# Forming the low parts of the projection weights with adding DMAs instead of a VectorE subtraction

## The chip, the core and the metric

The kernel runs on one core of a Trainium2 chip. The metric is device time in microseconds of one execution. A core has a matrix engine (PE; its weight loads are shown as PEld), VectorE (DVE), ScalarE (ACT), GpSimd (POOL) and SyncE (SP), each working through its own queue in order and waiting at semaphores, and 16 DMA engines that all queues share.

## The reference

One decoder layer over 1024 tokens of width 1024, in float32. Cut to what matters here:

```
u = rms_norm(x, ln_g)
z = u @ w_in                       # 1024 x 7168: seven groups of 8 column blocks of 128
c_val, c_glu, c_gate, hq, hf, hi, hg = split(z)
y_conv = (silu(layer_norm(conv31(c_val * sigmoid(c_glu)))) @ w_pw2 + b) * silu(c_gate)
y_hgrn = rms_norm(gated linear recurrence of hq, hf, hi in chunks) * silu(hg)
h = x + concat(y_conv, y_hgrn) @ w_out
h = h + sigmoid(rms_norm(h) @ w_pg) * (p @ w_pp)
out = rms_norm(h)
```

## The kernel before

Every large product is made of three matmuls in the rounded type float32r: each operand is split into `hi`, the operand rounded to float32r, and `lo`, the operand minus `hi`; then hi·hi + hi·lo + lo·hi are summed in PSUM. So a weight block needs its hi and its lo before its product can begin: the first matmul reads `w..h`, and the third already `w..l`.

The stages: a start (load `p`, `x` and the parameters, project `p` into `pe_d`, normalise and transpose `x` into the tiles `uh`, `ul`); the z stage, which makes `z` block by block, with the convolution and the recurrence of each head woven between; the pointwise projection; the output projection; the gated embedding.

In the z stage a weight block is 128 columns of `w_in`, 512 KB, in SBUF as 128 partitions of 1024 numbers. `ztile(idx)` prepares block `wz<idx>` (48 of them), and `values` prepares two blocks `wv_0`, `wv_1` for two heads at a time (8 in all). Both call `prep`: SP loads the block into a tile of tag `raw`, ACT writes `hi` by a copy, and DVE writes `lo` by a subtraction. The tags `raw`, `hi` and `lo` of the pool `wp` have three buffers each. So the load of a block waits until the block three before it has been split, and the split of a block waits until PE has finished the product of the block three before it. All of this stands at a raised priority (`high_priority(2000)`), so the scheduler places it early.

The order on each engine is set by the tile framework's scheduler, with offsets from the kernel: the last steps of a head (`ro`, `on`, `ot`) and of a convolution group (`ry`, `yn`) are placed later by hand. `rstd_of` makes the factors `rx` (rows of x), `ry` (convolution) and `ro` (heads) with two small POOL instructions each; the head's factor goes POOL `ro`, ACT `on`, PE transposes `ot`.

At the start SP's queue holds, in this order, the loads of `p`, `wpp`, the first block `wz8`, rows of `x` (`xt`), three more blocks `wz0`, `wz32`, `wz48`, more rows of `x`, and then the small parameter rows (`prow`: `conv_w` with 31 rows of 4 KB, and eight more, the last of them `lb_logits`). The transposes `pt` on PE need all of `prow`, and PE's work on `x` stands behind `pt`.

Of the kernel before, what the change touches and what calls it, by code (L numbers as in the profile page):

```python
# [16 lines left out]
P = 128  # L17
T = 1024          # tokens
D = 1024          # model width
G = 8             # channel groups, heads, 128-row blocks of T and D  # L20
TAPS = 31
PAD = TAPS - 1
H = 512           # half a row of 1024: one PSUM bank of float32
EPS = 1e-6
# Order of the work of each head and channel group: projections of the GLU gate (u), conv value
# (c), forget gate (f), query (q), values of two heads (v), output gate (g); conv (C); HGRN (H).
ORDER = ("ucfgqvCH", "ucfgqCH") * (G // 2)
# How much later than traced the scheduler takes work that waits on a chain of small steps.
LATER_STATS, LATER_CONV, LATER_HEAD = 50, 330, 240
# columns of the transposed parameter table  # L30
R_CB, R_CG, R_CBETA, R_BPW, R_L0, R_L1, R_ON, R_LN, R_PE = range(TAPS, TAPS + 9)
# [4 lines left out]
def trunk_kernel(ctx: ExitStack, tc: tile.TileContext, x, p, ln_g, w_in, conv_w, conv_b,  # L36
# [25 lines left out]

    # ---------------------------------------------------------------- constants
    ident = cst.tile([P, P], F32, name="ident")
# [5 lines left out]

    # per-channel parameters, channels on partitions
    par = cst.tile([P, G, NR], F32, name="par")
# [3 lines left out]
    def load_params(work):  # L76
        rows = work.tile([NR, D], F32, name="prow")
        nc.sync.dma_start(rows[0:TAPS, :], conv_w[0])
        for r, ap in ((R_CB, conv_b), (R_CG, cnorm_g), (R_CBETA, cnorm_b), (R_BPW, b_pw2),
                      (R_ON, onorm_g), (R_LN, ln_g), (R_PE, pe_norm_g)):  # L80
            nc.sync.dma_start(rows[r:r + 1, :], ap)
        nc.sync.dma_start(rows[R_L0:R_L0 + 2, :], lb_logits)
        pt = bank("t", "pt")
        for g in range(G):
            nc.tensor.transpose(pt[:, g * NR:(g + 1) * NR], rows[:, g * P:(g + 1) * P],
                                ident[:NR, :NR])
        nc.vector.tensor_copy(par, pt[:, :G * NR].rearrange("p (g r) -> p g r", r=NR))
        # lower bound: first row of the softmax over the layers
        l0, l1 = par[:, :, R_L0], par[:, :, R_L1]
        mx = cst.tile([P, G], F32, name="lmx")  # L90
        e0 = cst.tile([P, G], F32, name="le0")
        e1 = cst.tile([P, G], F32, name="le1")
        nc.vector.tensor_tensor(mx, l0, l1, op=ALU.max)
        nc.vector.tensor_tensor(e0, l0, mx, op=ALU.subtract)
        nc.vector.tensor_tensor(e1, l1, mx, op=ALU.subtract)
        nc.scalar.activation(e0, e0, AF.Exp)
        nc.scalar.activation(e1, e1, AF.Exp)
        nc.vector.tensor_tensor(e1, e0, e1, op=ALU.add)
        nc.vector.reciprocal(e1, e1)
        nc.vector.tensor_tensor(lbt, e0, e1, op=ALU.mult)  # L100
        nc.vector.tensor_scalar(oml, lbt, -1.0, 1.0, op0=ALU.mult, op1=ALU.add)
# [10 lines left out]
    def split(hi, lo, src):  # L112
        nc.scalar.activation(hi, src, AF.Copy)
        nc.vector.tensor_tensor(lo, src, hi.bitcast(F32), op=ALU.subtract)

    def prep(src, shape, name):
        """A weight block: loaded, and split exactly into two float32r parts."""
        raw = wp.tile(shape, F32, tag="raw", name=name)
        nc.sync.dma_start(raw, src)
        hi = wp.tile(shape, F32R, tag="hi", name=name + "h")  # L120
        lo = wp.tile(shape, F32R, tag="lo", name=name + "l")
        split(hi, lo, raw)
        return hi, lo

    def colblock(w, c0):
        return w[:, c0:c0 + P].rearrange("(k p) c -> p k c", p=P)
# [3 lines left out]

    # ---------------------------------------------------------------- z phase
    uh = [[None] * G, [None] * G]
    ul = [[None] * G, [None] * G]
    with tc.tile_pool(name="st", bufs=1) as st:
        # layer embedding, projected: kept in DRAM until the gate is known
        KP = p.shape[1] // P
# [29 lines left out]
        def norm_x(hf, xs):  # L166
            """Normalised input of four token blocks, channels on partitions, split."""
            for k in range(G):
# [12 lines left out]
        load_params(st)  # L181
        # masks[l][s, col]: where the key s is one that the score column couples to, the columns
        # being those of the block of 32 that s lies in
        ones = st.tile([P, 4 * 48], F32, name="ones")
        nc.gpsimd.memset(ones, 1.0)

        def block_mask(dst, first, step_n, step_j, l):
            """Sets dst[s, n, j, i] where s is in the l keys from first + n step_n + j step_j."""
            src = ones[:, :dst.shape[1] * dst.shape[2] * l].rearrange(
# [9 lines left out]
        def own_block(name, mf):  # L199
            """The columns of each row's own block out of those of the four blocks of 32."""  # L200
            n = mf.shape[1] // 4
# [33 lines left out]
    def product(wh, wl, mh, ml, tag, name):  # L235
        """Two banks [128 columns of w, 512 tokens] of w^T m."""
        res = []
# [9 lines left out]
    def ztile(idx):  # L247
        with tc.high_priority(2000):
            wh, wl = prep(colblock(w_in, idx * P), [P, G, P], f"wz{idx}")
        return product(wh, wl, uh, ul, "z", f"z{idx}")  # L250

    def values(idx, vt):
        """Two column tiles of z with tokens on partitions."""
        with tc.high_priority(2000):
            ws = [prep(w_in[j * H:(j + 1) * H, idx * P:(idx + 2) * P]
                       .rearrange("(k p) c -> p k c", p=P), [P, 4, 2 * P], f"wv{idx}_{j}")
                  for j in range(2)]
# [22 lines left out]
    def hgrn(h, QD, K, F, vt, sgT):  # L280
        A, B = AT[h % 2], AB
        # Decayed scores. A level couples the later blocks of l tokens in a parent block to the
        # earlier ones: queries carry the decay since their block of l began (and over the
        # blocks in between), keys the decay until their block of l ends, so that every factor
        # is at most one.
        # Levels within blocks of 32: every block's scores take 48 columns, on its own 32
        # partitions, and go to B[s, chunk, t mod 32].
        blocks = T // 32

        def scores(l, rhs):  # L290
            pt = bank("t", f"sc{h}_{l}")
            pv = pt[:, :G * 48].rearrange("p (c w) -> p c w", c=G)
            for b in range(blocks):
# [4 lines left out]

        # Diagonal and pairs: the keys are the same.
        q01 = QD[:, :, :32].rearrange("p b (n j two) -> p b n j two", j=4, two=2)  # L300
# [9 lines left out]
                                  pv[:, :, 32:])  # L310
        # queries of a level of four blocks: per parent, its blocks 0..3, then 2 and 3 decayed
        # over one more block, then 3 over two more
        Q = wk.tile([P, 7 * T // 4], F32, tag="Q", bufs=2, name=f"Q{h}_2")
# [4 lines left out]
        def pair_keys(l, Fl):  # L318
            """Widens the keys' blocks from l to 2l; the decay over each block of 2l."""
            n = T // (2 * l)  # L320
# [9 lines left out]
        for l in (2, 8):  # L330
# [14 lines left out]
            for d0, j0, cnt in ((1, 0, 3), (2, 3, 2), (3, 5, 1)):  # L345
# [4 lines left out]
                    pv[:, :, :, js])  # L350
            # widen to blocks of 4l
            Q4 = wk.tile([P, 7 * T // 4], F32, tag="Q", bufs=2, name=f"Q{h}_{4 * l}")
# [24 lines left out]
        for l in (32, 64):  # L377
# [14 lines left out]
            Fl = pair_keys(l, Fl)  # L392
        # state after each chunk
        kt = wk.tile([P, G, P], F32, tag="kt", name=f"kt{h}")
# [145 lines left out]

    # ---------------------------------------------------------------- pointwise projection
    yp = ctx.enter_context(tc.tile_pool(name="yp", bufs=32, reuse_waits="tile"))
# [33 lines left out]

    # ---------------------------------------------------------------- output projection
    hs = [hp.tile([P, D], F32, name=f"h{tb}") for tb in range(G)]
# [3 lines left out]
    def accumulate(zs, hf, k, wh, wl, first, last):  # L582
        """zs: {(token block, column half): bank}."""
        for b in range(4):
# [34 lines left out]
    def norm_T(hf):  # L619
        """Scaled residual of 4 token blocks, channels on partitions, split; its RMS in rs."""  # L620
        hh = [None] * G
# [34 lines left out]

    # ---------------------------------------------------------------- gated layer embedding
    gh = [[None] * G, [None] * G]
# [8 lines left out]
    for tb in range(G):  # L667
# [5 lines left out]
        ot = wp.tile([P, D], F32, tag="lo", name=f"ot{tb}")  # L673
        # the last block ends in narrower pieces, so that less work follows the last product
        pieces = (H, H) if tb < G - 1 else (H, H // 2, H // 2)
# [54 lines left out]
```

## Time and profile before

| | |
|---|---|
| device time, 3 runs | 1147.01, 1147.38, 1149.27 us; median 1147.38 |
| span of the profiled execution | 1146.5 us; the page gives no time of its own for that execution beside it, so 0.9 us of the median lie around the span |
| PE, busy | 1124.8 us, 98% of the span |
| DVE, ACT, POOL, busy | 739.5, 443.0 and 72.0 us |
| DMA | 104.6 MB, 28.1% of 16 engines |

A stage is read by the share of it in which PE is busy, and by what ended PE's idle time. An idle engine that is not waited for costs nothing.

### The profile page before, as it was taken

The page shows a single profiled execution, that of the slowest core. Times are in us where ns is not written, and L with a number is a line of the kernel's source. Part 1 is how long each engine was busy: PE and PEld are TensorE (multiplying, and loading weights), DVE is VectorE, ACT ScalarE, POOL GpSimd, SP SyncE. Part 2 cuts the span into 40 slices and gives each one's busy share as a digit, 9 for nine tenths or more (in the row PEclk, how much of TensorE's full clock was granted, in tenths as well). Part 3 has the DMA queues.
Part 4 walks back from the last instruction along what each step waited for, and adds up shares of the span by engine and source line. Part 5 has one row for each costly group of instructions (what it writes and reads, how often), then busy time and mean ns, then how long its engine had stood idle before and what let it go on. Part 6 is the DMA issues. An engine that isn't in the chain of part 4 may idle for free.

```text
span 1146.5 us, 17744 instructions
## 1 busy us (share of the span) xinstructions
PE 1124.8 (98%) x7408; PEld 945.6 (82%) x7408; DVE 739.5 (65%) x1145; ACT 443.0 (39%) x811; POOL 72.0 (6%) x107
## 2 busy tenths in 40 slices
PE   6999999999999999999999999999999999999997
PEld 4888978889888789788898788888888888887886
DVE  3659579998499996599993896242334325226444
ACT  4823244253354442344532632442123324126333
POOL 3100001001001010010010010000000001001000
PEclk9899999999999999999999999999999999999999
DMA  7611121211111112111111112277335632334221
GB/s 247 236 37 55 37 66 30 74 55 39 55 57 56 59 35 74 56 37 56 57 56 56 57 56 93 74 242 254 110 92 165 195 99 77 107 109 149 92 92 56
DMA packets 85715, 104.60 MB, mean 91 GB/s; under 512 B 3290, under 2 KB 65754, under 8 KB 85634
## 3 DMA queue, kind: packets, MB, share of 16 engines
q1 hardware_dynamic: 85634, 103.46, 28.1%
q8 instruction: 58, 0.95, 0.3%
q14 instruction: 23, 0.19, 0.1%
HBM read 82.48 MB, written 20.97 MB: 90 GB/s over the span
## 4 chain that ended last, share of the span: by engine, by line
PE 89%; DVE 6%; DMA 2%; ACT 1%; issue 1%; SPq 0%; POOL 0%; POOLq 0%; ACTq 0%
PE z L241 14%; PE z L242 14%; PE z L243 14%; DVE y L452 4%; PE v L264 3%; PE v L265 3%; PE v L263 3%; PE pg L683 3%; PE pg L684 3%; PE pg L682 3%; PE oA L591 3%; PE pw L243 3%; PE pw L241 3%; PE oA L589 3%; PE oA L588 3%; PE pw L242 3%
## 5 line engine op out<-in xcount | busy, mean ns | idle before, releaser
L452 DVE SCALAR_TENSOR_TENSOR y<-vpad,par,y 128x1024 f32<-128x1024 f32 x232 | 288.8, 1278 | 1.1
L682 PE MATMUL pg<-gh,hh 128*128 128x512 f32 (+1 forms) x136 | 51.4, 378 | 0.0
L683 PE MATMUL pg<-gl,hh 128*128 128x512 f32 (+1 forms) x136 | 51.4, 378 | 0.0
L684 PE MATMUL pg<-gh,hl 128*128 128x512 f32 (+1 forms) x136 | 51.3, 377 | 0.0
L519 DVE TENSOR_TENSOR vpad<-z,gl 128x512 f32<-128x512 f32 x16 | 11.0, 691 | 42.7 <-PE z L243 42.7
L263 PE MATMUL v<-wv_0h,uh 128*128 128x256 f32 x128 | 36.7, 287 | 0.0
L265 PE MATMUL v<-wv_0h,ul 128*128 128x256 f32 x128 | 36.5, 285 | 0.0
L264 PE MATMUL v<-wv_0l,uh 128*128 128x256 f32 x128 | 36.5, 285 | 0.0
L263 PE MATMUL v<-wv_1h,uh 128*128 128x256 f32 x128 | 36.2, 283 | 0.0
L264 PE MATMUL v<-wv_1l,uh 128*128 128x256 f32 x128 | 36.2, 283 | 0.0
L265 PE MATMUL v<-wv_1h,ul 128*128 128x256 f32 x128 | 36.2, 283 | 0.0
L266 ACT ACTIVATE vt<-v 128x256 f32<-128x256 f32 x32 | 12.2, 382 | 58.9 <-PE v L265 58.9
L688 DVE TENSOR_TENSOR gt<-gt,pet 128x512 f32<-128x512 f32 (+1 forms) x17 | 11.2, 661 | 36.1 <-ACT gt L687 36.1
L108 POOL TENSOR_SCALAR ro<-sso 128x8 f32<-128x8 f32 x8 | 8.4, 1054 | 389.9 <-ACT on L129 389.9
L475 DVE TENSOR_SCALAR y<-yt,mv,ry 128x128 f32<-128x128 f32 x64 | 23.5, 404 | 13.1 <-POOL ry L109 13.1
L570 DVE SCALAR_TENSOR_TENSOR sgr<-pw,par,sgr 128x512 f32<-128x512 f32 x16 | 12.0, 750 | 30.1 <-PE pw L243 30.1
L437 ACT ACTIVATE on<-o,ro 128x128 f32<-128x128 f32 x64 | 18.5, 386 | 29.0 <-POOL ro L109 29.0
L682 PEld LDWEIGHTS pg<-gh,hh 128*128 128x128 f32 x136 | 25.6, 188 | 4.7
L683 PEld LDWEIGHTS pg<-gl,hh 128*128 128x128 f32 x136 | 25.6, 188 | 4.7
L684 PEld LDWEIGHTS pg<-gh,hl 128*128 128x128 f32 x136 | 25.6, 188 | 4.5
L483 ACT ACTIVATE yc<-yn,par 128x512 f32<-128x512 f32 x16 | 12.5, 778 | 39.8 <-PE yn L482 39.8
L129 ACT ACTIVATE on<-o 128x128 f32<-128x128 f32 x64 | 16.9, 278 | 23.3 <-PE up L409 18.9
(802 smaller groups left out, 3463.6 us busy)
## 6 DMA issues: line engine op xcount, KB each, us to landing
wz<-in_w_in_dram SPq DMA_DIRECT2D x48, 512.0 KB
wo<-in_w_out_dram SPq DMA_DIRECT2D x32, 512.0 KB
xt<-in_x_dram SPq DMA_DIRECT2D x8, 512.0 KB
pe_d<-pes SPq DMA_DIRECT2D x8, 512.0 KB
wv<-in_w_in_dram SPq DMA_DIRECT2D x8, 512.0 KB
yc_d<-yc SPq DMA_DIRECT2D x8, 512.0 KB
yh_d<-sgT SPq DMA_DIRECT2D x8, 512.0 KB
sg_d<-sgc SPq DMA_DIRECT2D x8, 512.0 KB
```

The source lines that it names most:

```text
L241: mm(z, lhsT=wh[:, k, :], rhs=mh[hf][k], start=k == 0, stop=False)
L242: mm(z, lhsT=wh[:, k, :], rhs=ml[hf][k], start=False, stop=False)
L243: mm(z, lhsT=wl[:, k, :], rhs=mh[hf][k], start=False, stop=k == G - 1)
L263: mm(z, lhsT=uh[hf][k][:, c], rhs=wh, start=k == 0, stop=False)
L264: mm(z, lhsT=uh[hf][k][:, c], rhs=wl, start=False, stop=False)
L265: mm(z, lhsT=ul[hf][k][:, c], rhs=wh, start=False, stop=k == G - 1)
L452: nc.vector.scalar_tensor_tensor(y[j % 2], vp[:, j:j + T], pcol(g, j), y[j % 2], op0=ALU.mult, op1=ALU.add)
L588: mm(z, lhsT=mixh[hf][k][:, c], rhs=wh[j], start=first, stop=False)
L589: mm(z, lhsT=mixh[hf][k][:, c], rhs=wl[j], start=False, stop=False)
L682: mm(z, lhsT=hh[k][:, c], rhs=gh[j][k][:, o:o + w], start=k == 0, stop=False)
L683: mm(z, lhsT=hh[k][:, c], rhs=gl_[j][k][:, o:o + w], start=False, stop=False)
L684: mm(z, lhsT=hl[k][:, c], rhs=gh[j][k][:, o:o + w], start=False, stop=k == G - 1)
```

## The change

The 56 weight blocks of the z stage are prepared by a new function. ACT writes both tiles from the raw block: `hi` as before, and into `lo` the raw block times -1, rounded to float32r by the tile's type, that is, minus `hi`. Then POOL issues a DMA that adds the raw block onto `lo` where it lies in SBUF, which leaves raw minus `hi`. The blocks of the later stages, and `wpp`, keep `prep`. The rest of the diff takes comments out.

```
+    def prep_by_dma(src, shape, name):
+        raw = wp.tile(shape, F32, tag="raw", name=name)
+        nc.sync.dma_start(raw, src)
+        hi = wp.tile(shape, F32R, tag="hi", name=name + "h")
+        lo = wp.tile(shape, F32R, tag="lo", name=name + "l")
+        nc.scalar.activation(lo, raw, AF.Copy, scale=-1.0)
+        nc.scalar.activation(hi, raw, AF.Copy)
+        nc.gpsimd.dma_start(out=lo, in_=raw, accum_op=ALU.add)
+        return hi, lo
...
     def ztile(idx):
         with tc.high_priority(2000):
-            wh, wl = prep(colblock(w_in, idx * P), [P, G, P], f"wz{idx}")
+            wh, wl = prep_by_dma(colblock(w_in, idx * P), [P, G, P], f"wz{idx}")
         return product(wh, wl, uh, ul, "z", f"z{idx}")
...
         with tc.high_priority(2000):
-            ws = [prep(w_in[j * H:(j + 1) * H, idx * P:(idx + 2) * P]
+            ws = [prep_by_dma(w_in[j * H:(j + 1) * H, idx * P:(idx + 2) * P]
                        .rearrange("(k p) c -> p k c", p=P), [P, 4, 2 * P], f"wv{idx}_{j}")
                   for j in range(2)]
```

The first place is SP's queue at the start, from the block `wz8` to the first parameter rows; `wz` rows load weight blocks, `xt` rows load rows of `x`. Before:

```order
L119 DMA wz8_608<-in_w_in_dram 128x8x128
L157 DMA xt0_162<-in_x_dram 128x1024
L157 DMA xt1_171<-in_x_dram 128x1024
L119 DMA wz0_666<-in_w_in_dram 128x8x128
L119 DMA wz32_724<-in_w_in_dram 128x8x128
L119 DMA wz48_785<-in_w_in_dram 128x8x128
L157 DMA xt2_180<-in_x_dram 128x1024
L157 DMA xt3_189<-in_x_dram 128x1024
L78 DMA prow_198<-in_conv_w_dram 31x1024
```

The same place after the change:

```order
L128 DMA wz8_608<-in_w_in_dram 128x8x128
L168 DMA xt0_162<-in_x_dram 128x1024
L168 DMA xt1_171<-in_x_dram 128x1024
L128 DMA wz0_667<-in_w_in_dram 128x8x128
L128 DMA wz32_726<-in_w_in_dram 128x8x128
L168 DMA xt2_180<-in_x_dram 128x1024
L128 DMA wz48_788<-in_w_in_dram 128x8x128
L168 DMA xt3_189<-in_x_dram 128x1024
L78 DMA prow_198<-in_conv_w_dram 31x1024
```

The load of `wz48`, the fourth block, takes the raw buffer of `wz8`; it has moved behind one load of `xt`, and it waits for the adding DMA of `wz8` where it waited for the subtraction.

The second place is POOL's queue in the z stage, around the factors of the first heads. Before, it holds nothing but these factors (`ry`, `ro`):

```order
L108 TENSOR_SCALAR ry0_1186<-mv0_1157 128x8
L109 TENSOR_TENSOR ry0_1186<-ry0_1186,mhalf_102 128x8
L108 TENSOR_SCALAR ro0_1447<-sso0_1421 128x8
L109 TENSOR_TENSOR ro0_1447<-ro0_1447,mhalf_102 128x8
L108 TENSOR_SCALAR ry1_1833<-mv1_1804 128x8
```

After the change the adding DMAs stand between them:

```order
L108 TENSOR_SCALAR ry0_1193<-mv0_1164 128x8
L109 TENSOR_TENSOR ry0_1193<-ry0_1193,mhalf_102 128x8
L133 DMA wz49l_1666<-wz49_1663 128x1024
L133 DMA wz25l_1725<-wz25_1722 128x1024
L133 DMA wz10l_2138<-wz10_2135 128x1024
L133 DMA wz2l_2197<-wz2_2194 128x1024
L108 TENSOR_SCALAR ro0_1454<-sso0_1428 128x8
L109 TENSOR_TENSOR ro0_1454<-ro0_1454,mhalf_102 128x8
L133 DMA wz34l_2256<-wz34_2253 128x1024
L108 TENSOR_SCALAR ry1_1845<-mv1_1816 128x8
```

Each of these DMAs waits on POOL for ACT's copies of its block, and what stands behind it waits too; `ro0` now stands behind the DMA of `wz2`, and the DMA of `wz34` behind `ro0`.

## Rows read from the trace of the kernel before

**Rows 1.** The page: busy time of each engine, share, instructions.

```profile
PE 1124.8 (98%) x7408; PEld 945.6 (82%) x7408; DVE 739.5 (65%) x1145; ACT 443.0 (39%) x811; POOL 72.0 (6%) x107
```

**Rows 2.** Busy us by stage: PE, PEld, DVE, ACT, POOL; clock, DMA share, GB/s.

```profile
0.00:49.00 49.00, 37.21 (x167) 30.36 (x168) 24.46 (x41) 31.06 (x54) 16.96 (x43) 0.93 0.75 250
49.00:782.00 733.00, 731.33 (x5622) 619.33 (x5621) 565.95 (x896) 294.38 (x564) 43.18 (x32) 1.00 0.22 67
782.00:1035.00 253.00, 253.00 (x1134) 209.89 (x1133) 95.47 (x116) 71.56 (x101) 2.99 (x8) 1.00 0.40 127
```

**Rows 3.** The chain that ended last, at the start: start, us, what.

```profile
11.89 1.23 DVE wz8l L114
13.13 0.37 SPq L119
...
15.58 10.40 DMA prow<-in_conv_w_dram
26.00 1.57 DMA prow<-in_lb_logits_dram
```

**Rows 4.** Timeline of PE, two waits at the start (in brackets).

```profile
28.03 1.04 PE L85 MATMUL pt<-ident,prow 40*128 40x40 f32 x8 [4.65 <-DMA prow<-in_lb_logits_dram]
...
47.71 1.53 PE L171 MATMUL ut<-ident,xt 128*128 128x128 f32 x12 [1.05 <-DVE xt L162]
```

**Rows 5.** Busy time by stretch at the start: the DMA share stands next to last.

```profile
13.00:18.00 5.00, 5.00 (x21) 4.10 (x20) 3.41 (x6) 3.95 (x9) 1.93 (x4) 1.00 1.23 299
18.00:21.00 3.00, 3.00 (x15) 2.48 (x14) 0.00 (x0) 1.48 (x2) 0.00 (x0) 1.00 0.87 336
21.00:26.00 5.00, 2.38 (x11) 1.65 (x9) 1.51 (x2) 1.40 (x4) 1.71 (x4) 1.00 0.06 25
```

**Rows 6.** Timeline of ACT at the start.

```profile
10.76 1.06 ACT L113 ACTIVATE wz8h<-wz 128x1024 fp32r<-128x1024 f32 x1 [0.61 <-DMA wz<-in_w_in_dram]
```

**Rows 7.** One block's split, and PE's first use of its low part.

```profile
127.21 1.06 ACT L113 ACTIVATE wz1h<-wz 128x1024 fp32r<-128x1024 f32 x1 [1.06 <-PE v L265]
...
140.46 0.19 PEld L243 LDWEIGHTS z<-uh,wz1l 128*128 128x128 f32 x1
```

**Rows 8.** The same for the block with the least time.

```profile
94.51 1.07 ACT L113 ACTIVATE wv_1h<-wv 128x1024 fp32r<-128x1024 f32 x1 [4.62 <-PE z L242]
...
106.85 0.19 PEld L264 LDWEIGHTS v<-wv_1l,uh 128*128 128x128 f32 x1
```

**Rows 9.** Busy time by stretch: a store of yc alone, a load of wz alone.

```profile
161.00:165.00 4.00, 4.00 (x137) 3.25 (x138) 4.00 (x10) 3.81 (x6) 0.00 (x0) 1.00 0.35 134
186.00:190.00 4.00, 4.00 (x24) 3.44 (x23) 4.00 (x6) 2.17 (x16) 0.00 (x0) 1.00 0.44 131
```

**Rows 10.** Timeline: the factor of the first head and of the last.

```profile
183.71 1.06 ACT L113 ACTIVATE wz2h<-wz 128x1024 fp32r<-128x1024 f32 x1 [6.65 <-PE z L242]
...
190.20 1.18 POOL L108 TENSOR_SCALAR ro<-sso 128x8 f32<-128x8 f32 x1 [55.30 <-ACT on L129]
191.46 2.56 POOL L109 TENSOR_TENSOR ro<-ro,mhalf 128x8 f32<-128x8 f32 x1
...
194.06 1.66 ACT L437 ACTIVATE on<-o,ro 128x128 f32<-128x128 f32 x6 [3.94 <-POOL ro L109]
...
194.72 0.14 PEld L441 LDWEIGHTS ot<-ident,on 128*128 128x128 f32 x1
...
732.02 0.20 POOL L108 TENSOR_SCALAR ro<-sso 128x8 f32<-128x8 f32 x1 [34.82 <-ACT on L129]
732.30 1.64 POOL L109 TENSOR_TENSOR ro<-ro,mhalf 128x8 f32<-128x8 f32 x1
```

**Rows 11.** Groups by line: VectorE's largest group.

```profile
L452 DVE SCALAR_TENSOR_TENSOR y<-vpad,par,y 128x1024 f32<-128x1024 f32 x232 | 288.8, 1278 | 1.1
```

## Prediction

> **What bounds the kernel now.** I read the page first, then the busy time by stage, then the chain of work that ended last, then the DMA share at the start. PE is busy 98% of the span [rows 1]. By stage [rows 2], the z stage, where all the changed blocks but the first are prepared, has PE busy for 731.33 of 733.00 us, and the two projections behind it for all of 253.00 us. DVE's share there does not matter by itself: PE waits for DVE, ACT and DMA together no more than 1.67 us in the whole z stage. The idle time of PE lies at the start: 11.79 of the first 49.00 us. There the chain [rows 3] runs from the subtraction `wz8l` on DVE to SP, which can only then issue the load of `wz48`, then two loads of `xt`, then `conv_w`; this load takes 10.40 us to land, `lb_logits` behind it 1.57 us, and PE's transposes `pt` wait 4.65 us for it [rows 4]. The DMA share says why 10.40 us [rows 5]: the engines are full to about 21 us with the blocks queued ahead, and from 21 to 26 us the share is 0.06, one engine of sixteen, which carries the 31 rows of `conv_w` alone. So whatever delays `conv_w` in SP's queue delays `pt`. Nothing behind it gives the time back: the later rows of `x` are loaded by the same queue behind it, PE has 1.05 us of waiting left before the z stage [rows 4], and that wait moves along.
>
> **What is removed.** 56 subtractions of 1.23 us on DVE [rows 3], 69 us of 739.5 [rows 1]. They stood beside PE's work; PE can get back at most the 1.67 us that it waits in the z stage, and most of those waits are for other things (transposes, scores). I take 0; bounds 0 and -1.7.
>
> **What is added on ACT.** 56 copies of 1.06 us [rows 6, 7], 59 us; ACT goes from 443 [rows 1] to about 502 us, 44%. A copy delays what stands behind it on ACT by about 1 us, the start of a convolution among them; on DVE 1.23 us goes away at about the same places, so the steps of the recurrence meet PE's matmuls about when they did. At the start it delays the rounding of `p` by 1 us, which is covered by PE's later wait of 4.65 us. I take 0; bounds -0.5 and +1.
>
> **What is added on the DMA engines: the price of one adding DMA.** The trace has none, so it is bounded. The wire: a store of 512 KB from SBUF in rows of 4 KB takes 0.35 x 4.00 = 1.4 us of all engines, a load of a `wz` block 0.44 x 4.00 = 1.8 us [rows 9]. The adding DMA reads two tiles and writes one. The lower bound is one such stream, 1.4 us; the upper is three, 4.2 us; I take two, 2.8 us, since reads and writes of a plain copy already overlap and only a second read is new. The latency: 1.57 us, the whole time of the 8 KB load of `lb_logits` [rows 3], of which I count 1.1 ahead of the data and 0.5 behind. POOL's issue: at least 0; at most 2.56 us, POOL's longest instruction in the z stage [rows 10]; I take 1.0, nearer the short end since the descriptors are few (128 rows). Together 1.0 + 1.57 + 2.8 = 5.4 us, bounds 3.0 and 8.3.
>
> **In the z stage it is covered.** A block's low part must be there when PE loads it. For `wz1` the two copies on ACT end at 127.21 + 2 x 1.06 = 129.3, and PE wants the low part at 140.46 [rows 7]: 11.1 us for the adding DMA. The same holds for `wz3`, `wz5` and `wz7` in the later heads. The first `wv_1` has least: 94.51 + 2 x 1.07 = 96.6 to 106.85 [rows 8], 10.2 us; worked out alike, the other 51 blocks have more than these five. With 5.4 us, and even with 8.3, all of them are in time. The raw buffer comes free 4 to 7 us later than now, but the block that is loaded into it is split only when the product of the block that frees it is done, and a load takes 1.8 us of wire and 1.57 us of latency. If an adding DMA took D, over these limits, each of the four `wz` would cost D - 11.1 and the first `wv_1` D - 10.2.
>
> POOL's queue is in order, so each place where a factor and a DMA have changed neighbours was compared. `ro0` stands behind the DMA of `wz2`: ACT's copies end at 183.71 + 2 x 1.06 = 185.8, `ro0` starts at 190.20 [rows 10]; POOL has 4.4 us to issue. The DMA of `wz34` stands behind `ro0`, which ends at 194.0, before ACT's copies of `wz34`. Price 0, as long as an issue holds POOL under 4.4 us. Behind that limit the cover is thin: `on` follows `ro` at once, and PE loads `ot` 0.66 us after `on` begins [rows 10], some 0.3 us after its first piece is done.
>
> **At the start it is on the path.** SP now holds `wz48`, `xt3` and `conv_w` until the adding DMA of `wz8` has landed. ACT's copies end at 10.76 + 2 x 1.06 = 12.9 [rows 6]; POOL has done its masks by then and waits; with POOL's 1.0 and 1.1 of latency the data start at 15.0. Before, the five blocks ahead of `conv_w` were through at about 21 [rows 5]; `wz48` and `xt3` are held back (1.8 + 1.4 = 3.2 us), so the other three would be through at 17.8. From 15.0 on these 2.8 us share the engines with the 2.8 us of the adding DMA: both done at 20.6, landed at 21.1. Then SP issues; data of `wz48` start at 22.2, two blocks take 3.2, `conv_w` alone 5.0: 30.4 in place of 26.0. **Shift +4.4 us.** Lower bound (issue 0, one stream): the DMA lands at 17.3, the engines never run dry, and `conv_w` is later only by the added 1.4 us: +1.4. Upper bound (issue 2.56, three streams): data from 16.5, done at 22.0, landed 22.5, two blocks by 26.8 in place of 21: +5.8.
>
> A page bears on this price. The Trainium skill, "DMA: Bandwidth & Descriptors", section "Anatomy of one DMA — SWDGE (gpsimd) path", fits a DMA issued from POOL by 2.0 us plus the bytes at 436 GB/s, an estimate of 3.2 us for 512 KB where I have 5.4; by it the DMA would land near 17.3 and the sum would be the lower bound, +1.4 us. No run here shows such a DMA.
>
> **Sum.** 0 + 0 + 4.4 on the profiled execution, whose span is 1146.5 us; with the 0.9 us around it that is the median of 1147.4 that was measured, so **1151.8 us**. Its own range is 1147.4 + 1.4 - 0.5 = 1148.3 to 1147.4 + 5.8 + 1 = 1154.2.
>
> **Rivals.**
> *The adding DMA is one plain stream (not slower).* It reads, adds and writes at the rate of a store, and POOL's issue is short: the engines never run dry, shift 1.4, **1148.8 us**, within 0.2%. For it: the DMA engines carry 299 to 336 GB/s at that moment [rows 5] without slowing for having two kinds of transfer. Against: two tiles must be read. It decides below a shift of 2.3.
> *The adding DMA is slow.* At 10 us of wire in place of 2.8, D is 12.6: four `wz` lose 1.5, the first `wv_1` 2.4, in all 8.4 us, and the start shifts by 4.4 + 7.2 = 11.6: **1167 us**. For it: no row shows the adder's rate. Against: it would be seven times a store of the same bytes [rows 9].
> *POOL is held while it issues.* POOL's two instructions for `ro` take 1.18 + 2.56 us beside a busy DVE and 0.20 + 1.64 us when DVE is idle [rows 10]: beside DVE's convolution steps of 1.28 us [rows 11] a POOL instruction can stand until one of them ends. An issue that stood so five times would hold POOL for 6.4 us, 2.0 over its limit, and PE would lose 1.7 us at `ot` in each of seven heads, with the start at the upper bound: 1147.4 + 5.8 + 12 = **1165 us**. It decides at four such waits. Against: DVE's steps at that place leave no gaps, yet `ro` stood only once in each instruction.
> The Trainium skill has this rule under "SBUF — State Buffer", section "SBUF: two separate sides": descriptors of a POOL-issued DMA cannot be written while DVE holds the shared port. The two `ro` rows agree that POOL waits for DVE; whether issuing does, no run here shows.
> *PE gains from a lighter DVE.* It can gain 1.67 us at most, less than 0.2% even if the start cost nothing: **1146** us.
>
> **How the numbers follow.** 0.2% of the time is 2.3 us, about what a measurement of this kernel can tell from no change. Forecast (shift 2.3 to 6): 0.62. One plain stream: 0.20. Slow adder: 0.09. POOL held: 0.05. Lighter DVE: 0.04. Slower by over 0.2%: 0.62 + 0.09 + 0.05 = 0.76; within: 0.20 and most of the last, 0.22; faster: 0.02. The range reaches down to 1148.2, which takes in nearly all of the plain stream, and up to 1160, where only the two slow rivals lie beyond.
>
> **What would show it.** In the profile after: PE's wait ahead of `pt` grown from 4.65 to some 9 us, and the chain there passing through the adding DMA of `wz8` in place of `wz8l` on DVE; `conv_w` landing at about 30; the z stage as long as before (731 us of PE), with no wait of PE on a low part; DVE at 670 and ACT at 502 us; the adding queue's share near 56 x 2.8 us. I am wrong if `pt` starts before 30, if PE waits for `w..l` or `ot` in the z stage, or if the stages behind it change.

## The result, and the profile after

The changed kernel takes 1155.32 us (1154.95 to 1155.62), the kernel before 1147.38: slower by a ratio of 1.0066, 95% interval [1.0046, 1.0085]. Forecast were 1151.8 us and "slower", with a range up to 1160. The two profiled executions differ by 7.1 us (spans of 1146.5 and 1153.6):

| part of the span | forecast | measured |
|---|---|---|
| start, to the first matmul on `wz0` | +4.4 | +4.20 (61.90 to 66.10) |
| z stage, to the first matmul on `wpw0` | 0 | +2.18 (781.71 to 788.09, less 4.20) |
| projections and embedding, to PE's end | 0 | -0.46 (1139.19 to 1145.11, less 6.38) |
| end of the program | 0 | +1.2 |

The medians differ by 0.8 more. Where one execution has both a time and a span, some 1.7 us lie between them, in the kernel before too (1147.07 beside a span of 1145.3); so the profiled execution of before, with its 1146.5, was slower than the median (as was that of e9 below, by 2.3 us), and the 0.9 us "around it" were no property of the kernel.

The busy times and the adding queue on the page after (for the queue: packets, MB, share of 16 engines), to hold against [rows 1]:

```profile
PE 1125.2 (98%) x7408; PEld 944.3 (82%) x7408; DVE 673.6 (58%) x1089; ACT 494.1 (43%) x867; POOL 122.0 (11%) x163
...
q0 software_dynamic: 8064, 29.36, 13.8%
```

DVE lost 66 us and ACT gained 51, about as foreseen (670 and 502 us of busy time). 13.8% of the span on 16 engines is 159 us, 2.84 us for each of 56 DMAs: the 2.8 us of the wire were right, though no run tests the reason given for them, that only a second read is new. The chain that ended last, after, at the start, answers to [rows 3]:

```profile
12.00 0.95 ACT wz8l L131
12.95 0.31 issue
13.26 8.25 DMA wz8l<-wz
21.57 0.37 SPq L128
21.98 0.57 SPq L168
22.61 8.88 DMA prow<-in_conv_w_dram
31.50 1.54 DMA prow<-in_lb_logits_dram
```

It goes where the prediction led it: POOL issues at 13.26, the low part lands at 21.5 (forecast 21.1), only then does SP issue `wz48`, `xt3` and `conv_w`, which lands at 31.50 (forecast 30.4). In the timeline of PE, `pt` waits over twice as long as in [rows 4]:

```profile
33.50 1.04 PE L85 MATMUL pt<-ident,prow 40*128 40x40 f32 x8 [10.66 <-DMA prow<-in_lb_logits_dram]
```

That is 5.5 us later than before. But the wait of 1.05 us at `ut` [rows 4] is gone, so 4.20 arrive at `wz0`. In the z stage these are PE's waits (weight loads; line, releaser: us, times, longest), after:

```profile
PEld sc L306 <- issue: 5.4, 16, 0.4
PEld sc L306 <- DVE K L334: 4.3, 8, 0.6
PEld up L420 <- ACT kt L412: 2.6, 8, 0.3
```

and before:

```profile
PEld sc L295 <- DVE K L323: 4.7, 8, 0.7
PEld sc L295 <- issue: 2.7, 9, 0.4
PEld sc L295 <- ACT Q L362: 2.5, 7, 0.4
PEld up L409 <- ACT kt L401: 0.3, 1, 0.3
```

No wait on a `w..l` and none on `ot`. The score loads (`sc`) of these rows wait no more than before, 24 times and 9.7 us in place of 24 times and 9.9: the seven waits put down to `ACT Q` before stand under `issue` after. What is new is `up`, which waits for `kt` in each of eight heads where it did in one. These 2.3 us more are the z stage's loss. What is late ahead of them shows in the row of the convolution's steps after, against [rows 11]:

```profile
L463 DVE SCALAR_TENSOR_TENSOR y<-vpad,par,y 128x1024 f32<-128x1024 f32 x232 | 288.5, 1278 | 18.7 <-ACT y L460 17.7
```

DVE, with 1.23 us less to do ahead of these steps, now idles 17.7 us waiting for ACT's first step `y`. Timelines of ACT and of DVE in one head, after:

```profile
155.33 1.06 ACT L132 ACTIVATE wz25h<-wz 128x1024 fp32r<-128x1024 f32 x1 [8.44 <-issue]
156.30 1.04 ACT L131 ACTIVATE wz25l<-wz 128x1024 fp32r<-128x1024 f32 x1
157.24 1.23 ACT L460 ACTIVATE y<-vpad,par 128x1024 f32<-128x1024 f32 x1
...
158.51 6.57 DVE L463 SCALAR_TENSOR_TENSOR y<-vpad,par,y 128x1024 f32<-128x1024 f32 x5 [2.23 <-ACT y L460]
...
165.32 0.68 DVE L334 TENSOR_TENSOR K<-K,F 128x512 f32<-128x512 f32 x1
```

and before:

```profile
151.08 1.06 ACT L113 ACTIVATE wz25h<-wz 128x1024 fp32r<-128x1024 f32 x1 [9.34 <-PE z L242]
152.16 1.25 ACT L449 ACTIVATE y<-vpad,par 128x1024 f32<-128x1024 f32 x1
...
153.44 6.57 DVE L452 SCALAR_TENSOR_TENSOR y<-vpad,par,y 128x1024 f32<-128x1024 f32 x5
...
160.26 0.69 DVE L323 TENSOR_TENSOR K<-K,F 128x512 f32<-128x512 f32 x1
```

The steps start 5.07 us later and `K` 5.06, where the start accounts for 4.20: the convolution and the recurrence are 0.87 us late in this head, because before, `y` on ACT ran beside the subtraction on DVE, and now both copies of `wz25` stand ahead of it on one engine.

PE does not simply wait for these 0.87 us: its own order, which the scheduler sets, has changed with them. Timeline of PE in this head, from the transposes `ktp`, which ACT copies into `kt`, to the first `up`, before:

```profile
175.33 1.03 PE L399 MATMUL ktp<-ident,K 128*128 128x128 f32 x8
176.12 0.48 PE L243 MATMUL z<-uh,wz49l 128*128 128x512 f32 x1
176.44 0.40 PE L241 MATMUL z<-uh,wz49h 128*128 128x512 f32 x1
176.67 0.39 PE L242 MATMUL z<-ul,wz49h 128*128 128x512 f32 x1
176.90 0.38 PE L409 MATMUL up<-vt,kt 128*128 128x128 f32 x2
```

and after:

```profile
180.41 1.03 PE L410 MATMUL ktp<-ident,K 128*128 128x128 f32 x8
181.20 0.48 PE L252 MATMUL z<-uh,wz49h 128*128 128x512 f32 x1
181.69 0.49 PE L420 MATMUL up<-vt,kt 128*128 128x128 f32 x2
```

`ktp` stands four matmuls of `z` later in PE's order and does not wait for `K`, whose last step on DVE ended at 179.76. But one matmul of `z`, not three, is left between `ktp` and `up` to cover ACT's copy: `up` starts 0.49 us behind the matmul ahead of it, where the step was 0.23 before the change. That is the loss of some 0.3 us, in seven heads more than before. What the late `y` would cost with PE's order unchanged, no run shows.

At the end POOL drains its queue. Instances of the last lines' instructions (ns: least, median, most), after and before:

```profile
L736 POOLq DRAIN  x3: 34/102/5249, 1147.6 to 1153.4; - x3
```

```profile
L725 POOLq DRAIN  x3: 39/78/657, 1141.7 to 1146.2; - x3
```

The long one runs from 1147.6 to 1152.8, past SP's drains behind the last store, which end at 1151.7 and set the end before: the 1.2 us.

### The profile page after: what moved, and what is told of

The parts are those of the page before. It is cut to its first block, busy times and chain, and to the rows that moved or that the text cites. A ratio compares the mean times of both kernels' runs of the same rounds, so it can differ in the third digit from the quotient of the medians.

```text
span 1153.6 us, 17906 instructions
## 1 busy us (share of the span) xinstructions
PE 1125.2 (98%) x7408; PEld 944.3 (82%) x7408; DVE 673.6 (58%) x1089; ACT 494.1 (43%) x867; POOL 122.0 (11%) x163
## 3 DMA queue, kind: packets, MB, share of 16 engines
q0 software_dynamic: 8064, 29.36, 13.8%
## 4 chain that ended last, share of the span: by engine, by line
PE 85%; DVE 5%; issue 4%; DMA 3%; ACT 1%; SPq 0%; POOLq 0%; POOL 0%; ACTq 0%
PE z L253 13%; PE z L252 13%; PE z L254 12%; DVE y L463 4%; PE v L275 3%; PE v L276 3%; PE v L274 3%; PE pg L694 3%; PE pg L695 3%; PE pw L253 3%; PE pw L252 3%; PE pg L693 3%; PE oA L600 3%; PE oA L599 3%; PE oA L602 3%
## 5 line engine op out<-in xcount | busy, mean ns | idle before, releaser
L463 DVE SCALAR_TENSOR_TENSOR y<-vpad,par,y 128x1024 f32<-128x1024 f32 x232 | 288.5, 1278 | 18.7 <-ACT y L460 17.7
L477 DVE BATCH_NORM_STATS2 bs<-yt 128x6 f32<-128x128 f32 x64 | 16.3, 265 | 41.2 <-PE yt L473 41.2
L448 ACT ACTIVATE on<-o,ro 128x128 f32<-128x128 f32 x64 | 18.6, 386 | 28.7 <-POOL ro L109 28.7
```

The source lines that it names most:

```text
L463: nc.vector.scalar_tensor_tensor(y[j % 2], vp[:, j:j + T], pcol(g, j), y[j % 2], op0=ALU.mult, op1=ALU.add)
```

## Experiments

My theory after this: the start loses through `wz8` alone, the z stage through the second copy on ACT, the end through POOL. Rivals: the general load of 56 adding DMAs, in the start and in the z stage. A summary first (us; shifts are those of the first matmul on a tile in the profiled execution, against before; the last column counts waits of PE at `ot` of over 1 us):

| kernel | median, its before | ratio, 95% | at `wz0` | at `wpw0` | POOL's last DRAIN | `ot` |
|---|---|---|---|---|---|---|
| the change | 1155.32, 1147.38 | 1.0046 to 1.0085 | +4.20 | +6.38 | 5.25 | 0 |
| e1 | 1149.15, 1147.07 | 1.0005 to 1.0023 | -3.23 | -1.00 | 5.17 | 0 |
| e2 | 1153.84, 1147.07 | 1.0049 to 1.0073 | +4.87 | +4.80 | 0.75 | 0 |
| e3 | 1182.03, 1147.07 | 1.0288 to 1.0314 | -0.41 | +34.13 | 0.66 | 7 |
| e4 | 1152.40, 1147.16 | 1.0035 to 1.0060 | +4.58 | +4.21 | 4.60 | 0 |
| e5 | 1171.92, 1147.07 | 1.0190 to 1.0262 | -0.56 | +19.06 | 1.33 | 4 |
| e6 | 1159.48, 1147.16 | 1.0091 to 1.0118 | +8.69 | +10.69 | 5.25 | 0 |
| e7 | 1151.00, 1147.16 | 1.0023 to 1.0049 | +3.17 | +3.03 | 0.66 | 0 |
| e8 | 1173.62, 1147.16 | 1.0218 to 1.0246 | -1.46 | +28.18 | 1.33 | 2 |
| e9 | 1144.07, 1147.38 | 0.9964 to 0.9982 | -2.21 | -2.31 | 0.66 | 0 |
| e10 | 1151.68, 1147.38 | 1.0027 to 1.0052 | +0.13 | +2.31 | 5.25 | 0 |
| e11 | 1142.75, 1147.38 | 0.9951 to 0.9976 | -5.90 | -5.80 | 4.51 | 0 |
| e12 | 1142.65, 1146.74 | 0.9952 to 0.9979 | -6.24 | -6.35 | 0.66 | 0 |

e5 and e8 touch no block ahead of `wz0`; their shifts of -0.56 and -1.46 there show how far this column scatters by itself.

**e1, e2: the first block apart.** In e1 `form = prep if idx == G else prep_by_dma` in `ztile`; in e2 the other way round, `values` keeping `prep`.

> Only the first block, wz8, is prepared by the subtraction; the other 55 keep the adding DMA. Theory (the start waits for the adding DMA of wz8; the z stage loses to the second ACT copy; the end of the program costs about 2 us once POOL issues DMAs): PE's wait ahead of pt is back at 4.65 us and the start's 4.2 us are gone, the 2.2 of the z stage and the 2 at the end and around the span stay, so some 1151.1 us. Rival (the start is late for the general load of 56 adding DMAs): little changes, 1155 us.

> Only wz8 is prepared by the adding DMA, the other 55 by the subtraction. Theory: the whole 4.2 us of the start, nothing in the z stage, and the end's 2 us if one DMA issued by POOL is enough for them: 1153.6 us. Rival (the end's cost grows with the number of such DMAs): 1151.6 us, POOL's last DRAIN near 0.7 us. With the first experiment the two losses should add to that of the change, 7.9 us, plus the end's 2 us, which both have.

e2 has the start's loss whole (+4.87) and nothing in the z stage: `wz8` alone makes it, not the load of 56 DMAs. e1 keeps the z stage's loss (-3.23 to -1.00, +2.23) and the end's. It is 2 us better than I expected, since its start is 3.2 us shorter than before: a gain that I had not seen (e12, and the clock in the last section). The end fell between theory and rival: one DMA does not do it, 55 do. The DRAIN is 0.66, 0.75, 1.33, 5.17, 5.25 us behind 0, 1, 8, 55, 56 adding DMAs, 0.082 us for each. e2 also lost 1.3 us at the transposes of `h` in the embedding, which I did not follow.

**e3: both copies, no DMA.**

```
         nc.scalar.activation(hi, raw, AF.Copy)
-        nc.gpsimd.dma_start(out=lo, in_=raw, accum_op=ALU.add)
+        nc.vector.tensor_tensor(lo, raw, hi.bitcast(F32), op=ALU.subtract)
```

> ACT writes both copies of every one of the 56 blocks as in the change, but VectorE then overwrites the low part by the old subtraction and there is no adding DMA. Theory (the second copy on ACT delays the convolution's first steps): the z stage loses 2.2 us or a little more, since VectorE isn't lighter, and the start and the end lose nothing: 1149.6 to 1151 us. Rival (the z stage loses to the traffic of the adding DMAs): z stage as before, 1147.4 us.

**e5: the query blocks only.** `form = prep_by_dma if idx // G == 3 else prep`, `values` keeping `prep`.

> Only the eight query blocks wz24 to wz31, whose copies stand on ACT ahead of the convolution's first step in the next head, are prepared by the adding DMA. Theory: nothing at the start, the 2.2 us of the z stage nearly whole, and the end's 2 us: 1151.1 us. Rival (the z stage's loss is spread over all blocks, as traffic would make it): 8/56 of 2.2, so 0.3, and the end's 2: 1149.7 us.

Both missed by far, +35 and +25 us, and the reason is neither theory. PE, DVE and POOL at one head of e3, timelines of the three engines:

```profile
197.82 0.33 PE L452 MATMUL ot<-ident,on 128*128 128x128 f32 x1 [2.88 <-ACT on L448]
...
189.51 6.07 DVE L463 SCALAR_TENSOR_TENSOR y<-vpad,par,y 128x1024 f32<-128x1024 f32 x5
...
192.08 3.55 POOL L108 TENSOR_SCALAR ro<-sso 128x8 f32<-128x8 f32 x1 [56.66 <-ACT on L140]
195.72 1.65 POOL L109 TENSOR_TENSOR ro<-ro,mhalf 128x8 f32<-128x8 f32 x1
```

POOL's first `ro`, 0.20 us when DVE is idle [rows 10], does not get in until DVE's run of five steps ends at 195.58; then `ro`, `on` and `ot` are all late. PE stands 2.9 us, seven times, and the clock falls behind each wait (stretch from 197 to 203 of e3; the clock stands third from last):

```profile
197.00:203.00 6.00, 5.18 (x20) 4.08 (x21) 2.79 (x4) 3.81 (x10) 0.36 (x1) 0.72 0.00 0
```

So it is the thin cover that the rival "POOL is held" named, with `ro` itself held and no DMA in between. Beside this loss the z stage's waits in e3 and e5 are those of the changed kernel: `up` for `kt` 2.6 us in 8 heads, in both. And in both, as in the change, one matmul of `z` stands between `ktp` and `up` in every head; before and in e2 it is three in seven of the eight. So the loss comes with the copies (e3 has no adding DMA, and keeps the subtractions) and from the query blocks (e5 has no others). The rival, traffic, falls.

**e4: all but the query blocks.** `form = prep if idx // G == 3 else prep_by_dma`.

> The change, but the eight query blocks wz24 to wz31 keep the subtraction. Theory (the z stage's 2.2 us are the second copy of these blocks on ACT ahead of the convolution's first steps): the waits at the second score level and at the states are as before, the start's 4.2 us stay, and POOL's last DRAIN, which took 0.66, 0.75, 1.33, 5.17 and 5.25 us behind 0, 1, 8, 55 and 56 adding DMAs, takes 0.66 + 48 x 0.082 = 4.6 us: some 1152 us. Rival (the loss is spread over all blocks): 1154.5 us. POOL's two ro instructions may be held by VectorE's steps as in two of the runs ahead; then PE waits 2.7 to 3.1 us at ot in some heads.

1152.4 us. PE's waits in its z stage are those of before again, the one at `up` among them:

```profile
PEld up L421 <- ACT kt L413: 0.3, 1, 0.3
```

Eight or nine matmuls of `z` now stand between `ktp` and `up` in seven heads. No time is lost between `wz0` and `wpw0` with 48 adding DMAs there, and the DRAIN took 4.60 us as worked out.

**e8: is the loss of e5 the wait for `ro`?** e5 with `LATER_HEAD` 350 in place of 240.

> The experiment with the eight query blocks alone by adding DMA, with LATER_HEAD 350 in place of 240: on, ot of heads 1, 3 and 5 stand some 100 matmuls later on PE, those of heads 0, 2, 4 and 6 hardly. Theory (its loss of 25 us is PE waiting at ot for ro, which VectorE's steps hold on POOL, about 4 us for each head with the slow clock behind it): no wait at ot in heads 1, 3 and 5, waits left in 0, 2, 4 and 6 only: 1150 to 1166 us. Rival (the loss has to do with the DMA of the block and not with ro): as long as without the edit, 1164 to 1179 us.

`ro` was held 7.23 us in heads 1, 3, 4 and 6. PE waited at `ot` in 4 and 6 (3.9 us each), and not in 1 and 3, whose `ot` stood later: that far as the theory says. The total missed, since PE then lost 13.8 us at the first block of the pointwise projection, which I did not follow.

**e6, e7: the parameters by another queue.** In both, the nine loads of `load_params` are `nc.scalar.dma_start` in a `tc.high_priority(150)`; e6 is the change, e7 the kernel before.

> The change, with the nine loads of parameter rows issued by ACT at its start in place of SP. Theory (at the start only conv_w behind SP's wait costs time): PE's wait ahead of pt goes, the start's 4.2 us with it and part of the 4.65 us that the kernel before waits, the z stage's 2.2 us and the end's 1.2 stay: 1146 to 1148 us. Rival (the load of the adding DMAs delays x as well): PE waits at ut in place of pt, 1151 us or more.

> The kernel before, with the nine loads of parameter rows issued by ACT at its start. Theory: PE's 4.65 us at pt go, with the slow clock behind that wait, as far as x is there: 1142 to 1144 us, some 3.5 us under the same edit made to the change. Rival (x is late by then): 1146 us or more.

Both missed: the remedy was worse. With `conv_w` issued at the same moment as `p`, the load of `p` lands late, and PE's first work starts at 11.6 in place of 5.0 (timeline of PE in e7):

```profile
11.63 3.49 PE L145 MATMUL pT<-ident,prows 128*128 128x128 f32 x16 [11.63 <-DMA prows<-in_p_dram]
```

In e6 PE waits at `pt` (4.77) and at `ut` (5.29) as well. Whether `p` waited for the one engine that carries `conv_w` was not looked into; the order of the loads of `x` and of the blocks moved too, so this pair says little of the change.

**e9, e10: `conv_w` on more engines.** Nothing moves but one row on SP; e9 is the kernel before, e10 the change.

```
-        nc.sync.dma_start(rows[0:TAPS, :], conv_w[0])
+        nc.sync.dma_start(rows[0:16, :], conv_w[0][0:16, :])
+        nc.sync.dma_start(rows[16:TAPS, :], conv_w[0][16:TAPS, :])
```

> The kernel before, with conv_w loaded as 16 and 15 rows in place of 31; nothing else moves. Theory (pt waits for the 5 us in which one DMA engine of sixteen carries conv_w): both pieces land at about 22.5, pt starts near 23.5 in place of 28.0, and with the shorter wait the clock may not fall: 1140 to 1143 us. Rival (x is the next thing late and takes the gain): 1145 us or more, with a new wait of PE at ut.

> The change with the same edit. Theory (the start's loss is conv_w issued 7 us later, behind the adding DMA of wz8, and then alone on one engine): conv_w still issues at 22.6 but lands near 24.5, pt starts near 26.5 in place of 33.5, the 7 us come off: 1147 to 1149.5 us, still 5 to 7 us above the kernel before with the same edit, since SP's wait, the z stage's 2.2 and the end's 1.2 stay.

The Trainium skill, "DMA: Bandwidth & Descriptors", section "Why a DMA increments its semaphore by 16 and not by 1", says that a DMA runs on the largest number of engines up to 16 that divides its outermost size: one for 31 rows, 16 and 15 for the pieces. The runs agree: in before the DMA share is 0.06, one engine of sixteen, while `conv_w` lands [rows 5], and with the pieces `pt` starts at 24.90 in place of 28.03. In e9 PE's wait ahead of `pt` shrinks from 4.65 to 0.24 us, and the kernel is 3.3 us faster than before; the rival was half right, as PE waits 2.18 us for `xt` at `ut` instead. In e10 `pt` starts at 29.67 in place of 33.50, less than I hoped, since the small rows behind `conv_w` land late. The difference of the pair, 7.6 us, is that of the change: it does not hang on `conv_w` being slow, only on its being issued late.

**e11: both causes undone.** e10 with `form = prep if idx == G or idx // G == 3 else prep_by_dma`.

> The change with conv_w in two pieces and with the subtraction for wz8 and for the eight query blocks: 47 adding DMAs stay. Theory (start and z stage lose only through these nine blocks, the end by the count of DMAs): as the kernel before with conv_w in two, plus POOL's last DRAIN of 0.66 + 47 x 0.082 = 4.5 us, which is 0.5 past what SP's last store covers: 1140.5 to 1143.5 us. Rival (the 47 DMAs cost something of their own): 1145 us or more.

1142.75 us with 47 adding DMAs left: beyond the 0.5 us at the end that was foreseen they cost nothing of their own, and e11 is even 1.3 us under e9; in the profiled executions its start is shorter by 3.7. The last scaling of `xt` on DVE and POOL's work beside it, in the kernel before (timelines of the two engines):

```profile
44.88 1.85 POOL L273 MEMSET AT<- 128x1024 f32 x2
...
44.97 2.69 DVE L162 TENSOR_SCALAR xt<-xt,rx 128x1024 f32<-128x1024 f32 x1 [0.72 <-POOL rx L109]
```

and after the change:

```profile
52.06 0.90 POOL L133 DMA_DIRECT2D wz0l<-wz  x1 [1.90 <-ACT wz0l L131]
53.95 0.85 POOL L133 DMA_DIRECT2D wz32l<-wz  x1 [0.98 <-ACT wz32l L131]
54.49 2.16 POOL L284 MEMSET AT<- 128x1024 f32 x2
...
50.20 0.75 DVE L173 TENSOR_SCALAR xt<-xt,rx 128x1024 f32<-128x1024 f32 x1 [0.71 <-POOL rx L109]
```

These rows say why. The memsets, now behind two DMAs that wait for ACT, no longer meet the scaling, which takes 0.75 us in place of 2.69; PE's wait at `ut` goes.

**e12: the same without a DMA.** e9 with `nc.vector.memset(AT[i], 0.0)` for `nc.gpsimd.memset(AT[i], 0.0)`.

> The kernel before with conv_w in two pieces, as e9, and POOL's two memsets of AT done by VectorE, where they stand behind the last of the splits; no adding DMA, and nothing else moves. Theory (where the adding DMAs of wz0 and wz32 stand on POOL, they keep its memsets of AT, 1.85 us, off the last scaling of x on VectorE, which takes 2.67 us beside them and 0.75 without; this is what the version with both causes undone has over e9): the last scaling takes 0.75 to 1.3 us, PE's wait of 2.18 us at ut shrinks to under 0.5, and the time is that of the version with both causes undone, 1142 to 1143 us. Rival (that version gains from the subtractions taken off VectorE): the wait at ut stays, 1144 us.

```profile
40.42 0.89 DVE L163 TENSOR_SCALAR xt<-xt,rx 128x1024 f32<-128x1024 f32 x1 [0.71 <-POOL rx L110]
```

1142.65 us, and PE's wait at `ut` for `xt` is gone: that was the memsets' place, not the lighter DVE. e2, e3 and e5, whose memsets stand as before, keep a wait of 1.05 us there. In time the gain is small: each against its own before, e9 has 3.3 us and e12 4.1, and their intervals overlap. e11 and e12 beat both kernels by 4 us and more; e12 needs no adding DMA at all.

## Why the prediction was right, and where it was not

- **What is removed: right.** 56 subtractions less gave PE nothing. What the change did give, 1.05 us at `ut`, came from POOL's order (e12). The bound on it had no ground, though: PE's idle time between its first matmuls on `wz0` and on `wpw0` is 1.67 us before and 1.61 after, in a stretch that is 2.18 us longer. The ends of matmuls are modelled in the profile, so the lost time stands inside PE's busy time, 718.14 and 720.38 us; only the waits of its weight loads show it, 16.4 us in all before and 18.6 after.
- **The price of an adding DMA: right where it is on the path, a little high elsewhere.** 5.4 us were forecast. From issue to landing they take 4.46 to 8.25 us, median 4.64, of which POOL's issue is 0.83 to 1.05; the 8.25 is `wz8`, beside the loads of the start, where I had 8.2. The 3.2 us by the fit of the Trainium skill that the prediction named ("DMA: Bandwidth & Descriptors", section "Anatomy of one DMA — SWDGE (gpsimd) path") are under all 56.
- **Cover in the z stage, POOL's order: right.** No `w..l` was late, the issue of 0.85 us was far under the 4.4, and `ot` did not wait.
- **The start: right in sum, +4.2 for +4.4, by two errors.** `pt` was 5.5 us later, 1.1 more than worked out (the low part landed 0.4 late, the transfers behind it took 0.7 more). And "that wait moves along" was wrong: it vanished, because POOL's memsets moved behind two of the DMAs. I had compared POOL's queue at the factors and not at the start.
- **The step that failed: "What is added on ACT", 0 with an upper bound of +1.** It cost 2.2 us. I set the copy added on ACT against the subtraction removed on DVE as if both stood in one line, and took it that the recurrence would meet PE's matmuls about when it did. They ran side by side; the convolution's `y` stood behind ACT alone and came late (0.87 us in the head shown), and the scheduler gave PE another order, in which `up` follows `ktp` too closely (0.3 us, in eight heads where it was one). I had compared the orders of SP and POOL and not PE's.
- **A term that was not there: the end.** POOL's last DRAIN grows by 0.082 us with each adding DMA, to 5.25 us, of which 1.2 stick out.
- **The rivals.** The plain stream (1.4 us of wire) and the slow adder (10 us) fall with the measured 2.84 us. "POOL is held" did not happen to the DMAs' issues; in e3, e5 and e8, though, `ro` was held at just the place that it named, and there the z stage lost 20 to 35 us, more than that rival's 12.

## What to carry to other kernels

When work moves from one engine to another, set it against what stands behind it in each queue: an instruction added on ACT and one taken off DVE cancel only if the same thing waited for both. Then compare the order on every engine, PE's too, over the whole program, its first and last rows included: a schedule that is made anew can leave less work between a transpose and the matmul that needs its copy. A PE that is busy 98% of the time can still lose time inside its busy share; read the waits of its weight loads as well. And before paying for a wait at the start, ask why the transfer at its end is slow: two pieces of `conv_w` and a memset on another engine were worth some 4 us here.

## What the runs showed of the hardware that was not expected

- **POOL beside DVE's steps.** A POOL instruction of 0.20 us stood 1.02 to 7.23 us while DVE ran its steps `y` without a pause. The Trainium skill, "SBUF — State Buffer", section "SBUF: two separate sides", has the pair of ports that both use as a lock for a whole instruction; the runs agree, both ways (the memsets held DVE's scaling for 1.9 us). But POOL does not always get in when a step ends: in before it got in behind one step in each of seven heads, in e3 behind none until the run ended, and in e5 behind one step in three heads and not in four, though it asked 0.08 us after a step had begun in all seven. What decides is open. e5's time scattered from 1164.0 to 1178.8 us, where all others but e8 keep within 4.5.
- **An adding DMA's issue was not held by these steps**: 0.83 to 1.05 us in all 56, of which 24 ran beside them for most of their time.
- **The clock behind a short wait.** After the 4.65 us at `pt` the kernel before runs at half the clock, 1.2 GHz, for some 6 us; e1, after 3.00 us, does not, e5, after 2.89, does (clock 0.53 in the stretch shown here). Stretch from 28 to 34 us, before and e1 (clock third from last):

```profile
28.00:34.00 6.00, 5.97 (x30) 5.74 (x31) 3.78 (x11) 4.55 (x11) 0.00 (x0) 0.50 1.01 358
```

```profile
28.00:34.00 6.00, 5.29 (x42) 4.50 (x41) 4.28 (x12) 4.97 (x11) 0.00 (x0) 1.00 1.01 347
```

  How much of e1's shorter start is this and how much the memsets' place, was not told apart.
